# Attention with the two key blocks of a window laid over each other

## The chip, the cores and the metric

The kernel runs on one core of one Trainium2 chip. A core has five engines with queues of their own: TensorE (PE; its weight loads are shown apart as PEld), VectorE (DVE), ScalarE (ACT), GpSimd (POOL) and SyncE (SP, which here issues most DMA transfers). The metric is the device time of one execution in microseconds. Before the change it is 1674.65 us, the median of 3 runs (1673.33 to 1675.32).

## The reference, cut to what matters

One layer of a decoder trunk on 2048 positions of width 1024. A modulated input `u` is multiplied by a wide matrix and split into parts; one of them goes through sliding-window attention with 16 query heads of 64, 2 key/value heads, a bias by distance and one extra "sink" logit per head:

```python
in_window = (dist >= 0) & (dist < WINDOW)          # WINDOW = BLOCK = 128
...
logits = jnp.einsum('bnqhgd,bnkhd->bnhgqk', qb, kb).astype(jnp.float32) * (HEAD_DIM ** -0.5) + bias
logits = jnp.where(mask[None, :, None, None], logits, NEG_INF)
sink = jnp.broadcast_to(sinks.astype(jnp.float32).reshape(N_KV_HEADS, Q_GROUP, 1, 1),
                        logits.shape[:-1] + (1,))
probs = jax.nn.softmax(jnp.concatenate([logits, sink], axis=-1), axis=-1)[..., :-1]
out = jnp.einsum('bnhgqk,bnkhd->bnqhgd', probs.astype(v.dtype), vb)
```

Queries are taken in blocks of 128 and see the block before and their own, 256 keys. With a window of exactly 128, query `q` sees of the block before the keys at places `k > q`, and of its own block those at `k <= q`. So each place `k` from 0 to 127 is used once, either in the one block or in the other. The rest of the layer (gates, a causal pool over 2 to 16 positions, projections, a layer norm) is not touched by the change.

## The kernel before, in words

All large products are made in three passes of a split into a high and a low part (`hi`, `lo`: ACT casts the high part, DVE or POOL subtracts it, line 132 `low`), and by a scheme of sums and differences of matrix quarters, so that each weight tile `W` needs additions on POOL (`sum1` line 266, `mid` lines 270 and 271, `late` line 275) before it is split.

The work is staged: a head, a ring of products for the first 1024 positions (`first_phase`, with the keys and values among them), attention for these (`attention(ph, 0, ...)`, 801), the ring and attention for the second 1024 positions, and a last stage of projections and norms. The instructions of the wrapped engines (`pe`, `act`, `dve`, `pool`, `sp`, class `Ordered`) keep the order in which the program writes them on their engine; those written with `nc.` are placed by the planner.

An attention phase is a loop over `n`, with 64 turns that score and 3 more that finish. A turn stands for two heads and one query block; eight blocks, then the next two heads. Turn `n` writes, in this order:

- PE: the scores of turn `n` (`score_mms`, 992; two heads, high and low keys, 256 keys wide, into one PSUM tile `lg`); the transposes of the probabilities of turn `n - 2` (`turn_mms`, 1006; one per head and key block, into `pt`).
- DVE: the reciprocal of the sums of turn `n - 1`; additions of the output of turn `n - 3` (`o`).
- ACT: the scaling of one head of turn `n - 1`; the high part `pth` of `pt`.
- DVE and ACT: for each head of turn `n`, a reduction that adds the bias `bt` to the scores and finds the extreme (a custom DVE instruction that writes `L`), then the exponential with its sum.
- DVE: the low part `ptl` of `pt`; the scaling of the other head of turn `n - 1`.
- the fill (`filling`, 978): 5 or 6 quarter products, three matmuls of 128x512 each, of the other work that shares the phase. For them `split` (919) writes on ACT a cast, and on POOL or DVE a low part, and on POOL `mid` or `late`; the low part is on DVE for `T1` and for what `on_dve` lists, otherwise on POOL. A split is written three products ahead of its use.
- PE: the value product of turn `n - 2` (`value_mms`, 1013): for both key blocks, `pth` and `ptl` against `vv`, which holds the high and the low part of V side by side.
- what falls due (`run_coming`, 823): among it on POOL the causal pool's sums (`pool_sums`, 830: `nxt`, `fin`), its gate (`take_p`, 858) and the attention gate (`o` by `ag`).

In the first block of the sequence only one key block exists (`k0 = P`), and the turn works on half the columns.

The keys and values of the second kv head are kept in DRAM and loaded over the first at turns 28 to 33. `turn_v` (747) makes `vv` in the ring before: it transposes V, takes the high and low parts, and stores those of the second kv head. `bias_rows` (780) builds on POOL, at the start, one row per head of the bias by distance, filled up with 1e30 outside the window (`ET` = 384 long); `bias_tile` (812) reads it shifted by one per partition.

## Time and profile before

| | |
|---|---|
| median of 3 runs | 1674.65 us |
| the profiled execution's span | 1673.9 us |
| PE busy | 1642.9 us (98%) |
| DVE, ACT, POOL busy | 1205.2, 1024.4, 947.1 us |
| PE on the chain that ended last | 84% of the span |

The span runs from the first to the last instruction of the profiled execution; the median counts what lies around it too and is of other executions. A row of a group gives the engine, the operation, output and input tiles, the shapes, the count, the busy time, the mean time of one in ns, and the idle time ahead with what ended it. Matmuls overlap in the array, so the mean of one is longer than its share of the busy time. A row of a window gives the length and, for each engine, the busy time and the number of instructions, then the granted clock, the share of the DMA engines and GB/s.

### The profile page before, as it was taken

To read this page: it belongs to the slowest core of one execution; us is meant where nothing else is said; L and a number is where in the kernel's file an instruction comes from. 1 tells how busy PE (TensorE), PEld (TensorE's weight loads), DVE (VectorE), ACT (ScalarE), POOL (GpSimd) and SP (SyncE) were. 2 spreads that over 40 slices of the span, in tenths; PEclk is the share of its full clock that TensorE was granted. 3 is DMA by queue.
4 is the path that set the end of the run, shared out by engine and by line. 5 is a ranking of instruction groups with operands and counts; after the bars stand their busy time and mean duration, and the time that the engine had idled before them with its cause. 6 is when DMAs were issued, how large, how long until landed. Compare 5 with 4: busy or idle time off the path is not lost.

```text
span 1673.9 us, 24680 instructions
## 1 busy us (share of the span) xinstructions
PE 1642.9 (98%) x8058; PEld 1383.7 (83%) x8058; DVE 1205.2 (72%) x2156; ACT 1024.4 (61%) x2146; POOL 947.1 (57%) x710
## 2 busy tenths in 40 slices
PE   7999999999999999999999999999999999999997
PEld 6788888888888788888888888888888888888886
DVE  6945646777867767576467677678668897879877
ACT  4754547778777656335477777786656455544552
POOL 3343437585867837873375858588355643433442
PEclk9999999999999999999999999999999999999999
DMA  9588843343543578873432434435869696668443
GB/s 362 209 288 296 209 156 121 100 133 107 164 139 110 177 275 289 326 265 131 143 128 82 145 125 152 145 109 188 301 227 351 241 326 234 225 232 295 152 151 114
DMA packets 185970, 331.56 MB, mean 198 GB/s; under 512 B 18016, under 2 KB 43760, under 8 KB 185840
## 3 DMA queue, kind: packets, MB, share of 16 engines
q1 hardware_dynamic: 182720, 325.72, 56.8%
q10 hardware_dynamic: 3088, 4.23, 1.1%
q8 instruction: 64, 1.05, 0.3%
q14 instruction: 66, 0.54, 0.1%
q0 software_dynamic: 32, 0.02, 0.0%
HBM read 223.77 MB, written 109.28 MB: 199 GB/s over the span
## 4 chain that ended last, share of the span: by engine, by line
PE 84%; DVE 6%; DMA 4%; POOL 2%; issue 2%; ACT 2%; SPq 0%; POOLq 0%; DVEq 0%; ACTq 0%
PE mm L57 53%; PE lg L57 24%; PE pv L57 4%; PE pt L57 4%; DMA head_T<-in_wada_dram 1%; DVE w_set L132 1%; DMA set_T<-ain_T 1%; DVE wide L57 1%; DMA head_B<-in_wada_dram 1%; DVE set_T L57 1%; DVE L L57 1%; DVE w_set L57 0%; ACT L L57 0%; ACT w_set L57 0%; POOL W L270 0%
## 5 line engine op out<-in xcount | busy, mean ns | idle before, releaser
L57 PE MATMUL mm<-set_B,w_set 128*128 128x512 f32 x2664 | 652.1, 392 | 0.1
L57 PEld LDWEIGHTS mm<-set_B,w_set 128*128 128x128 f32 x2664 | 495.9, 188 | 101.9 <-DVE set_B L57 0.7
L57 PE MATMUL mm<-set_T,w_set 128*128 128x512 f32 x1824 | 454.9, 396 | 1.6 <-DVE mm L57 1.2
L57 PE MATMUL lg<-set_T,w_set 128*128 128x512 f32 x1704 | 409.7, 390 | 2.1 <-ACT set_T L57 0.5
L57 PEld LDWEIGHTS mm<-set_T,w_set 128*128 128x128 f32 x1824 | 337.5, 189 | 70.5 <-DVE mm L57 3.3
L57 PEld LDWEIGHTS lg<-set_T,w_set 128*128 128x128 f32 x1704 | 318.4, 188 | 71.9 <-DVE w_set L132 1.6
L132 DVE TENSOR_TENSOR w_set<-W,w_set 128x1024 fp32r<-128x1024 f32 x137 | 194.7, 1423 | 143.9 <-ACT w_set L303 135.3
L303 ACT CAST w_set<-W 128x1024 fp32r<-128x1024 f32 x137 | 144.0, 1051 | 186.2 <-PE mm L57 130.2
L266 POOL TENSOR_TENSOR W<-W,A 128x512 f32<-128x512 f32 x46 | 73.7, 1603 | 260.0 <-DMA A<-in_win_dram 63.6
L57 POOL TENSOR_TENSOR w_set<-W,w_set 128x512 fp32r<-128x512 f32 x120 | 159.0, 1333 | 109.2 <-ACT w_set L57 104.4
L57 DVE TENSOR_TENSOR o<-pv,o 64x128 f32<-64x128 f32 x256 | 72.0, 281 | 96.9 <-ACT o L57 93.6
L57 POOL TENSOR_TENSOR W<-W 128x512 f32<-128x512 f32 x82 | 110.9, 1366 | 52.4 <-DVE sm L57 25.4
L57 ACT ACTIVATE L<-L,nm 128x257 f32<-128x257 f32 (+1 forms) x256 | 127.1, 498 | 18.4 <-DVE nm L57 8.9
L275 POOL TENSOR_TENSOR W<-W 128x512 f32<-128x512 f32 x46 | 70.8, 1540 | 112.3 <-DVE w_set L132 97.6
L270 POOL TENSOR_TENSOR W<-W 128x512 f32<-128x512 f32 x44 | 77.4, 1763 | 83.1 <-DVE w_set L132 70.9
L57 DVE CUSTOM_DVE_ANT_0 L<-lg,bt,nsink 128x256 f32<-128x256 f32 (+1 forms) x256 | 111.6, 473 | 14.4 <-DMA pg<-pg_d 5.1
L57 ACT CAST w_set<-W 128x512 fp32r<-128x512 f32 (+1 forms) x165 | 101.4, 628 | 25.1 <-POOL W L57 14.5
L57 ACT COPY o<-pv 64x256 f32<-64x256 f32 x128 | 47.3, 369 | 71.7 <-PE pv L57 70.5
L57 POOL TENSOR_TENSOR spare<-spare 128x512 f32<-128x512 f32 x48 | 82.8, 1732 | 10.1 <-ACT spare L57 5.8
L57 DVE TENSOR_TENSOR ptl<-pt,pth 128x512 fp32r<-128x512 f32 (+1 forms) x128 | 85.7, 669 | 1.0 <-ACT pth L57 0.9
L57 ACT ACTIVATE L<-L,sm 128x256 f32<-128x256 f32 (+1 forms) x128 | 64.3, 502 | 36.0 <-DVE sm L57 35.6
L271 POOL TENSOR_TENSOR W<-W 128x512 f32<-128x512 f32 x44 | 68.1, 1548 | 29.2 <-DMA W<-in_win_dram 22.0
(234 smaller groups left out, 2408.3 us busy)
## 6 DMA issues: line engine op xcount, KB each, us to landing
W<-in_win_dram SPq DMA_DIRECT2D x42, 512.0 KB, 5.4
W<-in_win_dram SPq DMA_DIRECT2D x42, 256.0 KB, 4.0
A<-in_win_dram SPq DMA_DIRECT2D x42, 256.0 KB, 4.7
ag_d<-sig SPq DMA_DIRECT2D x32, 256.0 KB, 5.9
pg_d<-sig SPq DMA_DIRECT2D x32, 256.0 KB, 4.3
pg<-pg_d SPq DMA_DIRECT2D x32, 256.0 KB, 3.2
pin_B<-fin SPq DMA_DIRECT2D x32, 256.0 KB, 2.0
ag<-ag_d SPq DMA_DIRECT2D x32, 256.0 KB, 3.0
```

Of the source, the lines that this page charges most:

```text
L57: return lambda *args, **kw: self.tc.keep_in_program_order(op(*args, **kw))
L132: engine.tensor_tensor(dst, src, as32(hi), ALU.subtract)
L266: e.tensor_tensor(self.w[:, 1, :], self.w[:, 2, :], self.a22, ALU.add)
L270: e.tensor_tensor(x[:, 1, :], x[:, 1, :], x[:, 0, :], ALU.subtract)
L271: e.tensor_tensor(x[:, 2, :], x[:, 0, :], x[:, 2, :], ALU.subtract)
L275: e.tensor_tensor(x[:, 3, :], x[:, 3, :], x[:, 1, :], ALU.subtract)
L303: a.copy(by_two(hi), raw)
```

## The change

A query block's two score blocks are laid over each other before the softmax. A mask `own` (1 where `k <= q`) is made once; a predicated copy on DVE puts the own block's scores over those of the block before where the mask is 1, in PSUM. Bias rows, bias tiles, reductions, exponentials, scalings, transposes and the splitting into parts then work on 128 columns per head. In the first block (`c0`), the own block's scores are used alone with a bias that a select on POOL fills with 1e30 outside the window.

The value product is `p V_before + p_own (V_own - V_before)`: the probabilities `px` (high and low part) against `vv` of the block before, and `pm`, which is `px` with zeros where the key is not of the own block, against `dv`, the differences of neighbouring V blocks. `pm` is made by a select on POOL (`own_half`). `turn_v` also makes the differences and their parts, stores those of the second kv head, and they are loaded at turns 30 and 33. In the fill, the low parts of `B11` and `T4` are made on DVE for all products.

```diff
-ET = 384
+ET = 256
...
-            turn_v(ph, s, *vts[i])
+            turn_v(ph, s, *sorted(vts, key=lambda v: v[0])[i])
...
     def turn_v(ph, s, t, vt):
+        nonlocal dv
+        if t == 0:
+            dv = kvp.tile([P, 2 * NB, P], F32R, tag="dv", name="dv")
...
+        last = v_last.rearrange("p (a d) -> p a d", a=2)
+        whole, steps = (ph.c(x).rearrange("p (b a d) -> p b a d", b=NB, a=2) for x in ("vw", "vs"))
+        nc.scalar.copy(whole, vtp)
+        nc.gpsimd.tensor_tensor(steps[:, 1:], whole[:, 1:], whole[:, 0 : NB - 1], ALU.subtract)
+        nc.gpsimd.tensor_tensor(steps[:, 0], whole[:, 0], last, ALU.subtract)
+        nc.scalar.copy(last, whole[:, NB - 1])
...
+        for full, src, stored, first in ((vv, vtp, v_d, 1), (dv, steps, dv_d, 0)):
+            blocks = slice(first + NB * t, first + NB * (t + 1))
+            for kv in range(2):
+                dst = ph.c("v1", F32R).rearrange("p (b d) -> p b d", b=NB) if kv else full[:, blocks]
+                parts(dst, src[:, :, kv, :])
+                if kv:
+                    sp.dma_start(stored[s, :, blocks], as32(dst))
...
-            dst = ph.t.tile([P, 2, CH], F32R, tag="k1", bufs=1, name="k1") if kv else kk[:, :, c0 : c0 + CH]
+            dst = kvp.tile([P, 2, CH], F32R, tag="dv", name="k1") if kv else kk[:, :, c0 : c0 + CH]
...
+        def own_half(out, x, fill, blocks, turned):
+            pool.affine_select(
+                out=out,
+                in_=x,
+                compare_op=ALU.is_ge,
+                fill=fill,
+                base=0,
+                pattern=[[0, 2]] * blocks + [[turned, P]],
+                channel_multiplier=-turned,
+            )
...
-        on_dve = set()
+        on_dve = {(x, name) for x in range(K + 2) for name in ("B11", "T4")}
...
-        def turn_mms(L, k0):
-            pt = ps.tile([P, 2, 2, P], F32, tag="pt", bufs=1, name="pt")
-            for hf in range(k0 // P, 2):
-                for h in range(2):
-                    pe.transpose(pt[:, hf, h, :], L[:, h, hf * P : (hf + 1) * P], ident)
+        def turn_mms(L):
+            pt = ps.tile([P, 2, P], F32, tag="pt", bufs=1, name="pt")
+            for h in range(2):
+                pe.transpose(pt[:, h, :], L[:, h, 0:P], ident)
             return pt
 
-        def value_mms(b, k0, pth, ptl):
+        def value_mms(b, px, pm):
             pv = bank("pv")[:, 0 : 2 * P].rearrange("p (h q) -> p h q", h=2)
-            todo = [(hf, x) for x in (pth, ptl) for hf in range(k0 // P, 2)]
-            for n, (hf, x) in enumerate(todo):
-                mm(pv, vv[:, b + hf, :], x[:, hf], start=n == 0, stop=n == len(todo) - 1)
+            todo = [(x[:, u], m[:, b]) for x, m in ((px, dv if pm is None else vv), (pm, dv)) if x is not None for u in range(2)]
+            for n, (x, m) in enumerate(todo):
+                mm(pv, m, x, start=n == 0, stop=n == len(todo) - 1)
             return pv
...
-                pth = tp.tile([P, 2, 2, P], F32R, tag="pth", bufs=1, name="pth")
-                ptl = tp.tile([P, 2, 2, P], F32R, tag="ptl", bufs=1, name="ptl")
-                act.copy(pth[:, h0:], pt[:, h0:])
+                px = tp.tile([P, 2, 2, P], F32R, tag="px", bufs=1, name="px")
+                act.copy(px[:, 0], pt)
...
+                both, bt = lg[:, :, 0:P], bts[j]
+                if c0:
+                    both = lg[:, :, P:]
+                    bt = tp.tile([P, 2, P], F32, tag="pm", bufs=1, name="b0")
+                    own_half(bt, bts[j], BIG, 1, -1)
+                else:
+                    dve.copy_predicated(both, own, lg[:, :, P:])
                 for h in range(2):
                     dve.tensor_tensor_reduce(
-                        L[:, h, c0:256],
-                        lg[:, h, c0:],
-                        bts[j][:, h, c0:],
+                        L[:, h, 0:P],
+                        both[:, h],
+                        bt[:, h],
...
             if pt is not None:
-                low(dve, ptl[:, h0:], pt[:, h0:], pth[:, h0:])
+                low(dve, px[:, 1], pt, px[:, 0])
+                pm = None
+                if not k0:
+                    pm = tp.tile([P, 2, 2, P], F32R, tag="pm", bufs=1, name="pm")
+                    own_half(pm, px, 0.0, 2, 1)
...
             if pt is not None:
-                pvs[n - 2] = value_mms((n - 2) % U, k0, pth, ptl)
+                pvs[n - 2] = value_mms((n - 2) % U, px, pm)
...
+                sp.dma_start(as32(dv[:, 0:NB]), dv_d[s, :, 0:NB])
...
+                sp.dma_start(as32(dv[:, NB:]), dv_d[s, :, NB:])
...
+    nc.gpsimd.memset(own, 1)
+    nc.gpsimd.affine_select(
+        out=own, in_=own, compare_op=ALU.is_ge, fill=0.0, base=0, pattern=[[0, 2], [-1, P]], channel_multiplier=1
+    )
```

## The prediction

> **What bounds the kernel now.** First the page: TensorE (PE) is busy almost throughout, so time comes from PE's own work or from PE being made to wait.

> ```profile
> span 1673.9 us, 24680 instructions
> PE 1642.9 (98%) x8058; PEld 1383.7 (83%) x8058; DVE 1205.2 (72%) x2156; ACT 1024.4 (61%) x2146; POOL 947.1 (57%) x710
> ```

> Then the table by stage, for the two attention phases, from the first score product to the last value product (columns: window; length and PE busy; PEld, DVE, ACT, POOL busy; clock; DMA share; GB/s).

> ```profile
> 256.40:594.80 338.40, 334.75 (x1809) 287.51 (x1808) 244.69 (x668) 256.81 (x715) 247.64 (x200) 0.99 0.41 134
> 828.70:1174.10 345.40, 342.73 (x1870) 295.32 (x1871) 253.13 (x674) 262.11 (x717) 247.87 (x194) 1.00 0.41 135
> ```

> PE idles 3.65 and 2.67 us in 684. The other engines have room on average: POOL 73%, DVE 73%, ACT 76%. Each phase runs 64 score steps (67 turns of the loop); a turn takes 338.4/64.5 = 5.2 us. One turn in PE's timeline, and VectorE (DVE) in it:

> ```profile
> 446.60 0.40 PE L57 MATMUL pv<-pth,vv 128*128 128x256 f32 x2
> ...
> 447.07 0.63 PE L57 MATMUL lg<-kk,qs 128*128 128x256 f32 x4
> 447.54 0.60 PE L57 MATMUL pt<-ident,L 128*128 128x128 f32 x4
> 447.90 1.64 PE L57 MATMUL mm<-set_T,w_set 128*128 128x512 f32 x6
> 449.37 2.20 PE L57 MATMUL mm<-set_B,w_set 128*128 128x512 f32 x9
> 451.41 0.40 PE L57 MATMUL pv<-pth,vv 128*128 128x256 f32 x2
> ```
> ```profile
> 448.05 0.58 DVE L57 TENSOR_TENSOR o<-pv,o 64x128 f32<-64x128 f32 x2 [1.21 <-ACT o L57]
> 448.67 0.48 DVE L57 CUSTOM_DVE_ANT_0 L<-lg,bt,nsink 128x256 f32<-128x256 f32 x1
> ...
> 449.48 0.68 DVE L57 TENSOR_TENSOR ptl<-pt,pth 128x512 fp32r<-128x512 f32 x1
> ```

> Scores, transposes, 15 (or 18) fill products, value products, with no gap. The low half of the turned probabilities (ptl) is there at 450.16, PE wants it at 451.65: what prepares the value product has some 1.5 us to spare, no more.

> **The change part by part.** These are the groups that it touches, forms kept apart (busy us, mean ns), and three rows for its new POOL work.

> ```profile
> L57 PE MATMUL pt<-ident,L 128*128 128x128 f32 x496 | 75.5, 272 | 0.1
> ...
> L57 DVE CUSTOM_DVE_ANT_0 L<-lg,bt,nsink 128x256 f32<-128x256 f32 x240 | 106.7, 482 | 10.0 <-DMA pg<-pg_d 5.1 <-PE lg L57 1.2
> L57 DVE CUSTOM_DVE_ANT_0 L<-lg,bt,nsink 128x128 f32<-128x128 f32 x16 | 5.0, 348 | 4.4 <-DMA bt<-e_rep 4.2
> ...
> L57 DVE TENSOR_TENSOR ptl<-pt,pth 128x512 fp32r<-128x512 f32 x120 | 82.3, 686 | 1.0 <-ACT pth L57 0.9
> L57 DVE TENSOR_TENSOR ptl<-pt,pth 128x256 fp32r<-128x256 f32 x8 | 3.4, 419 | 0.0
> ...
> L57 DVE TENSOR_TENSOR w_set<-W,w_set 128x512 fp32r<-128x512 f32 x40 | 36.5, 914 | 23.6 <-ACT w_set L57 23.3
> ...
> L57 POOL TENSOR_TENSOR w_set<-W,w_set 128x512 fp32r<-128x512 f32 x120 | 159.0, 1333 | 109.2 <-ACT w_set L57 104.4
> ```
> ```profile
> masks.py:199 POOL TENSOR_SCALAR_AFFINE_SELECT ident<-ident x1: 291/291/291, 1.0 to 1.0; 128x128 f32<-128x128 f32 x1
> ```
> ```profile
> L1688 POOL MEMSET const-float32-0.0<- 128x1 f32 x1 | 0.1, 103 | 0.2 <-issue 0.2
> ...
> L57 POOL TENSOR_TENSOR fin<-fin,fix 128x16 f32<-128x16 f32 x8 | 2.1, 263 | 0.6
> ```

> Removed on PE: 120 turns have four transposes and keep two, the 8 turns of a first block have two already. 240 of 496 go, at 75.5/496 = 0.152 us of PE time each: **36.5 us**, all on the bounding engine, 0.30 us a turn. Scores keep their count and width. The value product has four products a turn before (hi, lo by two blocks) and four after (hi, lo by V, hi, lo by the difference): nothing.

> DVE, each turn: the two bias reductions lose 2 x (482 - 348) = 0.27 us, the low half 686 - 419 = 0.27. The predicated copy is not in the trace: between the 0.35 us of a 128x128 reduction and the 0.69 of a 512-wide subtraction from PSUM; I take 0.42, the 256-wide one. The chain to the low half becomes 0.12 us shorter, which by itself is off PE's path. ACT has less of everything (casts, exponentials, scaling of 128 columns for 256); it is not the bound, so nothing.

> New on POOL: one select of 512 elements in each of the 120 turns (`own_half` on px). The one select in the trace takes 0.291 us for 128. By proportion 512 cost 1.16; with the 0.263 that a tiny POOL operation takes as the fixed part, 0.37; with the 0.103 of the one-column memset, 0.103 + 4 x 0.188 = **0.86**, which I take, a select being the single-input kind. [...]

> Moved from POOL to DVE: the low halves of B11 and T4 in the fill, 25 a phase (14 + 13, less two already there). POOL loses 25 x 1.33 = 33 us and gains 60 x 0.86 = 52; it goes from 248 to 267 of some 330 us, 81%. DVE gains 25 x 0.91 = 23 and loses 60 x 0.12 = 7: 253 + 16 of 345, 78%. On average neither is a bound.

> But POOL runs its instructions in the order written, and **the select of turn n stands behind all that POOL got in the turns before it, and the value product of turn n now waits for it**. Before, PE needed POOL's results (fill low halves) only some two turns later, so a backlog cost nothing. From the turn shown: the low half is now there 2.97 us after the turn's start (450.16 - 447.07 = 3.09, less 0.12), the select at 3.9 with 0.05 to hand over. PE comes to the two masked products 0.30 us earlier than it came to the value product and 0.24 after it begins: 4.3 us in a 15-product turn, 5.0 in an 18-product one, 4.6 on average. So 0.7 us to spare, and between two selects POOL has 5.2 - 0.30 - 0.9 = 4.0 us for other work, 4.6-4.7 when the turn before was not held. What it has in one turn is uneven. Here are the stretches of POOL work in the first phase that the code issues in one turn (the second and the fourth: in two turns) and that exceed this; POOL busy is the fifth busy figure:

> ```profile
> 269.33:275.42 6.09, 6.09 (x36) 5.26 (x35) 4.27 (x11) 4.38 (x13) 6.08 (x6) 1.00 0.30 102
> 351.62:364.35 12.73, 12.73 (x74) 11.18 (x73) 7.90 (x23) 10.40 (x29) 12.42 (x12) 1.00 0.38 117
> 373.41:378.90 5.49, 5.49 (x32) 4.76 (x32) 4.37 (x12) 4.11 (x11) 5.49 (x5) 1.00 0.55 185
> 431.06:444.77 13.71, 13.51 (x74) 11.54 (x74) 11.40 (x31) 11.10 (x33) 12.28 (x12) 1.00 0.27 77
> 447.29:456.09 8.80, 8.80 (x50) 7.61 (x49) 7.94 (x19) 6.31 (x20) 8.64 (x9) 1.00 0.52 173
> 459.05:465.47 6.42, 6.42 (x36) 5.51 (x35) 4.69 (x17) 5.89 (x19) 6.34 (x7) 1.00 0.50 169
> 522.92:531.36 8.44, 8.44 (x51) 7.40 (x50) 5.88 (x17) 6.63 (x20) 8.13 (x9) 1.00 0.74 218
> 533.96:540.31 6.35, 6.35 (x40) 5.62 (x39) 5.00 (x11) 4.42 (x14) 6.11 (x7) 1.00 0.01 3
> 540.27:550.03 9.76, 9.50 (x51) 7.88 (x50) 7.99 (x23) 8.12 (x23) 9.37 (x10) 1.00 0.51 162
> 552.50:563.65 11.15, 11.15 (x60) 9.55 (x59) 8.21 (x19) 4.63 (x14) 10.91 (x10) 1.00 0.56 166
> ```

> PE is held by what is over 4.6 (8.6 for two turns; 4.0 for 540.27, right behind a held one), after taking off the moved low halves (two in 447.29 and 552.50, one in 522.92, at 1.33): 1.5 + 3.8 + 0.9 + 3.7 + 1.4 + 1.7 + 2.2 + 1.5 + 5.4 + 3.6 = 25.7 us. The second phase has the same order of work and as much POOL time: **51 us** in both.

> A hold also costs clock. Before, PE waited 2.0 us in all here:

> ```profile
> 567.02 0.50 PE L57 MATMUL pv<-pth,vv 128*128 128x256 f32 x2 [1.39 <-ACT pth L57]
> 568.15 0.51 PE L57 MATMUL pv<-ptl,vv 128*128 128x256 f32 x2 [0.63 <-DVE ptl L57]
> ...
> 569.56 5.27 PE L57 MATMUL mm<-set_T,w_set 128*128 128x512 f32 x15
> ```
> ```profile
> 570.00:572.00 2.00, 2.00 (x6) 1.57 (x5) 1.95 (x7) 1.65 (x4) 2.00 (x2) 0.50 0.70 265
> ```

> The granted clock fell to 0.50, and 15 products took 5.27 us for some 3.7 (1.64 + 2.20 in the turn shown, less overlap): 1.6 us more. Five holds a phase are of 2 us or over; while PE is slow POOL catches up, so half: 10 x 0.8 = 8, less the 3.6 us of this old wait and its clock, which the holds contain: 4.4. [...]

> The rest I cost at nothing. The mask and twice the bias operations at the start stand before POOL's first weight sum at 66 us, whose wait for its DMA covers them; the V differences in the stage before each attention (two PSUM copies, four POOL subtractions, two parts more a turn) lie under PE work that is 45.0 of 45 us busy there, and would cost up to 5 us a phase if the five c buffers ran out. The transfers of dv come at turns 30 and 33, four turns before use.

> **Sum:** 1673.9 - 36.5 + 51.4 + 4.4 = 1693.2 for the profiled execution, whose span lies 0.75 us under the median of 1674.65: **1694 us**.

> **The rivals.** *Holds that mostly vanish* (faster). POOL's operations are of two speeds for one form:

> ```profile
> 442.17 1.04 POOL L57 TENSOR_TENSOR fin<-nxt 128x512 f32<-128x512 f32 x1 [1.04 <-DMA pin_B<-fin]
> ```
> ```profile
> 537.70 1.30 POOL L57 TENSOR_TENSOR fin<-nxt 128x512 f32<-128x512 f32 x1
> ```

> If DVE's halved work lets most of them run at the quicker, the some 70 in the stretches (87 by the rows, less the moved ones and the neighbours cut by a window's edge) give back up to 70 x 0.26 = 18 us a phase, and a select at the lower end 12 x 0.5 = 6; then only the 540 stretch holds, and 1675 - 36.5 + 2 x 3 = 1644. It decides once POOL's work in a turn is below 4.6 us. For it: POOL averages under that. Against: the slow ones coincide also with DVE operations that stay. *DVE late* (slower still). A moved low half waits for ACT's cast, as the 23.3 us of waits in 40 of them show, 0.58 each, and stands ahead of the next turn's reciprocal. DVE's spare time is (338.4 - 244.7)/64.5 = 1.5 us a turn; where two fall into one turn (1.83 + 0.58) the low half comes 0.9 late. With half of the 50 exposed at (0.91 + 0.58): 37 us less the 0.7 spare in each: 1694 + 20 = 1714. *A wash*: holds and gain cancel, 1675; this would take holds of 36 us.

> **How the numbers follow.** Forecast 0.52 (its own range 1680 to 1712), holds vanish 0.27, DVE late 0.13, wash 0.08. 0.2% of 1675 is 3.3 us, about what a measurement can tell. Faster 0.27, same 0.08, slower 0.65. Low end 1646: just above the first rival. High end 1734: select at 1.16 (24 held turns x 0.3 = 7), DVE late, full clock loss (8).

> **What would show it.** Right: in the attention phases PE waits at `pv` for POOL `pm`, some 40 us or more, most at the turns listed; 256 transposes left; clock 0.5 in places. Wrong: PE waits for `pm` under 20 us; a select far from 0.86 us; waits at `pv` or the fill put down to DVE (px, w_set) instead; new waits in the stage of the V transposes.

## The result, and the profile after

The changed kernel takes 1736.3 us (median of 4 runs, 1734.3 to 1739.43) where the kernel before, in 4 runs beside it, takes 1674.28 us (1673.33 to 1675.32): a ratio of 1.037 (95% interval 1.0356 to 1.0385), 62 us slower. The prediction was 1694 us, slower; the direction is right, the size is three times the forecast.

The page of the changed kernel, with the chain that ended last by engine in the third row:

```profile
span 1734.3 us, 24556 instructions
PE 1646.5 (95%) x7818; PEld 1373.9 (79%) x7818; DVE 1216.8 (70%) x2335; ACT 965.0 (56%) x2162; POOL 988.6 (57%) x829
...
PE 31%; DVE 7%; POOL 6%; issue 4%; ACT 2%; DMA 1%; POOLq 0%; SPq 0%; DVEq 0%; ACTq 0%
```

240 matmuls are gone and PE is as long busy as before. The table by stage, the two attention phases (columns as in the prediction):

```profile
259.70:633.90 374.20, 341.18 (x1727) 287.03 (x1726) 253.10 (x755) 229.09 (x718) 259.00 (x241) 0.97 0.38 123
861.70:1234.10 372.40, 343.59 (x1742) 289.92 (x1743) 257.78 (x763) 228.84 (x718) 257.42 (x232) 0.97 0.38 124
```

Before, the phases took 344.0 and 345.5 us, so they are longer by 30.2 and 26.9. (The first window of the prediction's table, 338.4 us, stops 5.6 us short of that phase's last value product; the mean turn before is 5.2 us all the same.) The first score product starts at 259.7 us for 256.4 (+3.3), and the two stages behind the phases are within 0.6 us of what they were. PE idles 33.0 and 28.8 us in the phases, for 3.7 and 2.7. The view of waits says for what (columns: total us, times, longest):

```profile
PE pv L57 <- POOL pm L57: 45.6, 34, 5.3
PE mm L57 <- DVE mm L57: 13.9, 7, 2.5
POOL pm L57 <- DVE px L57: 100.7, 56, 6.6
```

The first is the wait that the prediction named: the value product for the masked probabilities. The third shows that POOL, at the same instruction, waits twice as long for its own input, in 56 turns: it is late in some turns and early in the others. The second wait is one that the forecast left out.

The groups that answer to those shown of before (busy us, mean ns, idle ahead):

```profile
L57 PE MATMUL pt<-ident,L 128*128 128x128 f32 x256 | 50.2, 278 | 0.0
...
L57 DVE COPY_PREDICATED lg<-own,lg 128x256 f32<-128x256 int8 x120 | 49.3, 410 | 3.9 <-PE lg L57 3.9
...
L57 DVE CUSTOM_DVE_ANT_0 L<-lg,bt,nsink 128x128 f32<-128x128 f32 x240 | 74.8, 349 | 4.5 <-DMA bt<-e_rep 0.2
...
L57 DVE TENSOR_TENSOR px<-pt,px 128x256 fp32r<-128x256 f32 x128 | 53.9, 421 | 0.3
...
L57 POOL TENSOR_SCALAR_AFFINE_SELECT pm<-px 128x512 fp32r<-128x512 f32 x120 | 80.8, 674 | 113.6 <-DVE px L57 100.7
```

The copy (0.42 forecast), the reductions and the low part are as costed. The select is 0.67, not 0.86. The transposes went from 75.5 us to 50.2, by 25.3 and not by 36.5.

Where a hold comes from, in the first phase: PE's two masked products of the turn that starts at 463.7 (listed in the prediction as 447.29:456.09), and POOL's order ahead of them:

```profile
470.13 0.50 PE L57 MATMUL pv<-pm,dv 128*128 128x256 f32 x2 [1.86 <-POOL pm L57]
```
```profile
464.60 1.30 POOL L57 TENSOR_TENSOR fin<-fin,pg 128x512 f32<-128x512 f32 x1 [3.26 <-DVE sm L57]
465.86 1.06 POOL L57 TENSOR_TENSOR nxt<-vb 128x518 f32<-128x518 f32 x1
466.99 1.05 POOL L57 TENSOR_TENSOR nxt<-nxt 128x516 f32<-128x516 f32 x1
468.12 1.37 POOL L57 TENSOR_TENSOR fin<-nxt 128x512 f32<-128x512 f32 x1
469.44 0.63 POOL L57 TENSOR_SCALAR_AFFINE_SELECT pm<-px 128x512 fp32r<-128x512 f32 x1
```

Four operations of the causal pool, which nobody needs at once, stand ahead of the select; POOL itself had been idle 3.26 us just before. The hold two turns earlier, and what the clock did behind both (windows; the clock is the third figure from the right):

```profile
456.53 0.50 PE L57 MATMUL pv<-pm,dv 128*128 128x256 f32 x2 [3.95 <-POOL pm L57]
...
457.48 4.58 PE L57 MATMUL mm<-set_B,w_set 128*128 128x512 f32 x12
```
```profile
457.80:461.00 3.20, 3.20 (x9) 2.43 (x9) 2.45 (x9) 1.86 (x7) 2.71 (x3) 0.50 0.49 168
...
471.40:474.40 3.00, 3.00 (x8) 2.32 (x7) 2.88 (x10) 2.34 (x8) 1.80 (x2) 0.50 0.10 39
```

In the two phases the clock falls to 0.50 ten times, eight times for 3.4 us and twice for 6.8 (before: once, for 3.4). PE works in 37.4 of these 40.9 us, so some 18.7 us of work are lost, for 1.7 before.

The second wait: PE wants the sum of a finished quarter (`close`, the row that ends on `mm<-mm,p`) out of the accumulator, and on DVE two moved low parts stand ahead of it, each of which waits for ACT's cast. PE first, then DVE:

```profile
611.07 1.50 PE L57 MATMUL mm<-set_T,w_set 128*128 128x512 f32 x3 [2.53 <-DVE mm L57]
```
```profile
607.70 1.60 DVE L57 TENSOR_TENSOR w_set<-W,w_set 128x512 fp32r<-128x512 f32 x1 [0.72 <-ACT w_set L57]
...
609.71 0.69 DVE L57 TENSOR_TENSOR w_set<-A,w_set 128x512 fp32r<-128x512 f32 x1 [0.41 <-ACT w_set L57]
610.32 0.69 DVE L57 TENSOR_TENSOR mm<-mm,p 128x512 f32<-128x512 f32 x1
```

The head, before and after: POOL builds the bias rows with twice the instructions, and ACT's cast into `set_T` comes 3.6 us later, after a wait that is new.

```profile
9.22 12.82 POOL L57 TENSOR_SCALAR head_T<-head_T 16x1 f32<-16x1 f32 x32 [7.56 <-DMA head_T<-in_relT_dram]
...
38.16 0.62 ACT L57 CAST set_T<-head_qs 128x512 fp32r<-128x512 f32 x1 [1.08 <-issue]
```
```profile
8.52 27.91 POOL L57 TENSOR_SCALAR head_T<-head_T 16x1 f32<-16x1 f32 x64 [6.55 <-DMA head_T<-in_relT_dram]
...
41.74 0.62 ACT L57 CAST set_T<-head_qs 128x512 fp32r<-128x512 f32 x1 [4.74 <-DMA e_d<-head_T]
```

The rows are built in a tile with the tag `set_T2` (`room` in `bias_rows`), so the cast that takes this space next has to wait until their transfer to `e_d` has read it.

### The profile page after: what moved, and what is told of

Same layout as the page of the kernel before. It is cut to its first block, busy times and chain, and to the rows that moved or that the text cites. A ratio compares the mean times of both kernels' runs of the same rounds, so it can differ in the third digit from the quotient of the medians.

```text
span 1734.3 us, 24556 instructions
## 1 busy us (share of the span) xinstructions
PE 1646.5 (95%) x7818; PEld 1373.9 (79%) x7818; DVE 1216.8 (70%) x2335; ACT 965.0 (56%) x2162; POOL 988.6 (57%) x829
## 4 chain that ended last, share of the span: by engine, by line
PE 31%; DVE 7%; POOL 6%; issue 4%; ACT 2%; DMA 1%; POOLq 0%; SPq 0%; DVEq 0%; ACTq 0%
PE mm L57 19%; PE lg L57 11%; POOL nxt L57 1%; POOL fin L57 1%; POOL W L57 1%; DVE w_set L135 1%; PE pv L57 1%; ACT L L57 1%; DVE qs L57 1%; POOL pm L57 1%; DVE wide L57 1%; DVE o L57 1%; DVE w_set L57 1%; ACT w_set L57 1%; POOL o L57 0%
## 5 line engine op out<-in xcount | busy, mean ns | idle before, releaser
L57 PE MATMUL mm<-set_B,w_set 128*128 128x512 f32 x2664 | 661.2, 396 | 0.9 <-DVE w_set L57 0.5
L57 PEld LDWEIGHTS mm<-set_B,w_set 128*128 128x128 f32 x2664 | 502.0, 190 | 106.2 <-DVE set_B L57 1.2
L57 PE MATMUL mm<-set_T,w_set 128*128 128x512 f32 x1824 | 460.3, 399 | 14.4 <-DVE mm L57 13.9
L57 PE MATMUL lg<-set_T,w_set 128*128 128x512 f32 x1704 | 410.6, 391 | 4.1 <-ACT w_set L57 2.2
L57 PEld LDWEIGHTS mm<-set_T,w_set 128*128 128x128 f32 x1824 | 339.9, 191 | 86.0 <-DVE mm L57 15.9
L57 PEld LDWEIGHTS lg<-set_T,w_set 128*128 128x128 f32 x1704 | 319.6, 188 | 73.7 <-ACT w_set L57 2.8
L57 POOL TENSOR_TENSOR w_set<-W,w_set 128x512 fp32r<-128x512 f32 x92 | 121.4, 1325 | 47.6 <-ACT w_set L57 47.4
L57 DVE TENSOR_TENSOR o<-pv,o 64x128 f32<-64x128 f32 x256 | 71.9, 281 | 108.4 <-ACT o L57 105.7
L57 POOL TENSOR_SCALAR_AFFINE_SELECT pm<-px 128x512 fp32r<-128x512 f32 x120 | 80.8, 674 | 113.6 <-DVE px L57 100.7
L57 ACT ACTIVATE L<-L,nm 128x129 f32<-128x129 f32 x256 | 101.4, 398 | 78.2 <-DVE nm L57 75.4
L57 DVE TENSOR_TENSOR w_set<-W,w_set 128x512 fp32r<-128x512 f32 (+1 forms) x73 | 80.0, 1096 | 71.9 <-ACT w_set L57 69.5
L57 POOL TENSOR_TENSOR W<-W 128x512 f32<-128x512 f32 x82 | 109.2, 1345 | 31.9 <-DVE w_set L57 19.7
L57 ACT CAST w_set<-W 128x512 fp32r<-128x512 f32 (+1 forms) x165 | 101.6, 628 | 29.8 <-POOL W L57 12.4
L57 ACT COPY o<-pv 64x256 f32<-64x256 f32 x128 | 47.3, 370 | 116.6 <-PE pv L57 115.1
L57 PE MATMUL pv<-pm,dv 128*128 128x256 f32 x240 | 53.9, 307 | 45.8 <-POOL pm L57 45.6
L57 POOL TENSOR_TENSOR spare<-spare 128x512 f32<-128x512 f32 x48 | 82.6, 1728 | 11.4 <-ACT spare L57 5.7
```

The source lines that it names most:

```text
L57: return lambda *args, **kw: self.tc.keep_in_program_order(op(*args, **kw))
```

## The experiments

All edits are against the changed kernel, and the diffs are shortened. The kernel before took 1674.3 to 1675.5 us beside each of them.

**1. Without the wait.** The masked products take `px` in place of `pm`; the selects still run, but nobody waits for them. The mask of the value product is left out of the computation.

```diff
-                pvs[n - 2] = value_mms((n - 2) % U, px, pm)
+                pvs[n - 2] = value_mms((n - 2) % U, px, pm and px)
```

> Changed kernel; the select still runs in every turn, but the last two value products of a turn take px in place of pm, so PE doesn't wait for POOL (the attention output leaves out the mask of the own block). Theory 'order' (PE is held because the select stands behind POOL's backlog): the 46 us of PE waits for pm go, and with them some 6 of the 10 drops of the clock (1.7 us each): 1736 - 46 - 11 = about 1679, 1670 to 1690. Rival 'load' (POOL has too much work, whoever waits for it): the fill's low halves come late in place of pm, and the time stays above 1715.

Measured: 1693.5 us (ratio 1.0113, 1.0098 to 1.0128), 3.5 us above the range of 'order' and far below the rival's 1715. The wait at `pm` and what hangs on it cost 43 us. PE still idles 18.3 and 15.6 us, now mostly for DVE:

```profile
PE mm L57 <- DVE mm L57: 17.5, 7, 6.9
```

**2. Without the selects too.** `own_half(pm, ...)` goes and `pm = px`; the same part is left out.

> As the run before, and the 120 selects are left out too (the attention output leaves out the mask of the own block). 'Order': within 6 us of the run that has the selects without the wait, 1670 to 1685. 'Load': 20 us or more below it. If DVE's waits (mm<-set_T waiting for a DVE addition, 14 us in the changed kernel) are of DVE's own making, they are still there.

Measured: 1682.2 us (1.004, 1.0025 to 1.0055), 11 us less than with the selects, between the two expectations. So the selects cost PE time beyond the wait for them; the fill's waits for DVE fall to 8.5 and 8.4 us from 12.6 and 10.8. One part of the path is in the two traces: the same DVE operations take 517.8 us in the phases with the selects and 505.9 without (the last section has more on this). How much of the 11 us it makes was not measured.

**3. And the low parts of B11 and T4 back on POOL**, the same part of the mask left out:

```diff
-        on_dve = {(x, name) for x in range(K + 2) for name in ("B11", "T4")}
+        on_dve = set()
```

> No select, and the low halves of B11 and T4 back on POOL (the attention output leaves out the mask of the own block). What is left of the change is fewer transposes and less work of DVE and ACT. If the two low halves in one turn on DVE make PE wait for DVE's additions: 15 to 22 us below the run without select (14 us of waits and some 4 drops of the clock), about 1655. If DVE's lateness came from POOL's selects: within 5 us of it.

Measured: 1660.0 us (0.9908, 0.9891 to 0.9925), 22 us less again, and faster than before. The phases:

```profile
260.20:596.25 336.05, 330.31 (x1727) 280.06 (x1726) 240.57 (x730) 229.28 (x720) 253.20 (x212) 0.99 0.42 137
825.30:1160.35 335.05, 330.23 (x1742) 281.09 (x1743) 243.51 (x738) 228.30 (x718) 248.18 (x194) 1.00 0.42 138
```

This is what laying the blocks over each other is worth if the mask costs nothing: 15 us, with 11 us of idle PE and the head's 3.8 (first score at 260.2 us) still in it.

**4. The low parts back on POOL, with the mask.** The changed kernel with the edit of 3 alone; the whole computation.

> Changed kernel with the low halves of B11 and T4 back on POOL, selects and waits as they are. 'Order': POOL has 50 x 1.33 = 66 us more ahead of its selects, in the turns of most work two operations more, PE waits for DVE 14 us less: 1736 + 40 - 20, 1740 to 1775. Rival 'DVE late' (the move is what costs): 1712 to 1725.

Measured: 1727.7 us (1.0317, 1.0302 to 1.0333), between the two expectations. The two effects of the move are both there and oppose each other: the waits for DVE's `close` nearly vanish, and those for `pm` grow from 45.6 to 54.1 us.

```profile
PE pv L57 <- POOL pm L57: 54.1, 34, 4.9
...
PE mm L57 <- DVE mm L57: 1.7, 2, 0.9
```

So the move to DVE did relieve POOL (by 8.5 us of waits) and cost more than that: 9 us net with the selects, 22 without them.

**5. The mask on DVE.** A multiplication by a tile of ones and zeros in place of the select, with the low parts back on POOL and the bias rows built once (as in 7); the whole computation.

```diff
-                    own_half(pm, px, 0.0, 2, 1)
+                    dve.tensor_tensor(pm, as32(px), keep, ALU.mult)     # keep repeated 4 times
```

> The whole computation. The mask of the own block is a multiplication on DVE (a 128x128 tile of ones and zeros, repeated) right behind the low half, in place of POOL's select; the low halves of B11 and T4 are back on POOL; the bias rows are built once and copied. Theory 'order': no instruction of POOL stands before the value product any more; against the run without select and with the low halves on POOL (1660) it has 120 DVE multiplications of about 0.69 us more, DVE at some 85% in the attention phases, and 3.5 us less in the head: 1656 to 1672, faster than the kernel before. Rival: DVE becomes the bound that POOL was, every turn 0.7 us late: over 1690.

Measured: 1702.1 us (1.0159, 1.0144 to 1.0174), above the rival's 1690. One multiplication takes

```profile
L57 DVE TENSOR_TENSOR pm<-px,keep 128x512 fp32r<-128x512 f32 x120 | 115.4, 962 | 4.1
```

and the waits for `pm` fall to 16.2 us, 28 times. The 42 us above experiment 3 are not all in waits that name the mask: 9.3 us are waits for `close` again, and 6.0 of them come in one turn of the first phase. In the two phases PE idles 35.2 us for 10.6, and its value products take 93.4 us for 83.6, its transposes 54.7 for 49.9. The 46 multiplications beside which POOL ran no two-input operation took the expected 0.69 us; the other 74 took 1.13 on average. So the mask on DVE is not free of POOL either.

**6. The value product later.** The select stays on POOL, and the value product goes behind the scores and transposes of the next turn, to give the select a turn's start more; low parts back, bias rows once; the whole computation.

```diff
-            if pt is not None:
-                pvs[n - 2] = value_mms((n - 2) % U, px, pm)
+            if n - 3 in ready:                     # right behind turn_mms of turn n
+                pvs[n - 3] = value_mms((n - 3) % U, *ready.pop(n - 3))
...
+                ready[n - 2] = px, pm
```

> The whole computation, select on POOL. The value product of a turn stands behind the next turn's scores and transposes (0.63 + 0.25 us of PE work later) in place of the end of its own turn; low halves back on POOL, bias rows built once. 'Order': each of the some 37 waits for pm gets 0.9 us shorter or goes: 54 - 30 = some 25 us of waits are left and half of the clock's drops; from 1727.7: 1727.7 - 30 - 8 - 3.5 = 1686, 1675 to 1698. Rival 'load': as the run with the low halves back, 1720 to 1728.

Measured: 1796.4 us (1.072, 1.0702 to 1.0738), missing both expectations. The edit brought waits of its own:

```profile
PE pv L57 <- DVE o L57: 107.2, 82, 3.2
```

The value product now writes the one `pv` bank just when DVE is about to add the one before to `o`, and ACT's next `px` waits for the product (145.2 us in 115 waits). The wait for POOL's `pm` did fall to 9.2 us, but with PE held elsewhere POOL has more time in any case, so this run does not test the theory. Putting the product a whole turn later would need second buffers of `px` and `pm`; it was not tried.

**7. The bias rows once.** One instruction per bucket, and a copy of the whole row; the whole computation.

```diff
-            for a in range(2):
-                pool.tensor_scalar(et[:, a, t0:t1], ...)
+            pool.tensor_scalar(et[:, 0, t0:t1], ...)
+        pool.tensor_copy(et[:, 1, :], et[:, 0, :])
```

> Changed kernel with the bias rows built once on POOL (32 small operations in place of 64) and copied. If the head's 3.3 us are ACT's wait for the DMA that reads the bias rows out of the space of set_T2: first score product near 256 us again and the whole 3 to 4 us shorter, 1732.5. Rival (the head's start varies with its DMA): no difference.

Measured: 1734.5 us (1.0353, 1.0337 to 1.0368). In the profile the first score is at 256.1 us again, 3.6 earlier, and the phases (373.7 and 372.3) stay. The medians differ by 1.8 us only, and the two ranges overlap, so the gain is shown in the profile and not in the time.

**8. Every transpose twice,** on top of experiment 3 (the mask left out): four transposes in a turn again.

```diff
-            for h in range(2):
+            for h in (0, 1, 0, 1):
                 pe.transpose(pt[:, h, :], L[:, h, 0:P], ident)
```

> The run without select and with the low halves on POOL (it leaves out the mask of the own block), with each transpose made twice into the same place: four per turn as before the change, and nothing else. It measures the disputed term. By the PE timeline (0.36 us from the first of four transposes to the next product, 0.14 of two) 128 turns cost 0.20 to 0.22 us each: 1660 + 26 to 28 = 1687. By the group's busy time over its count (the prediction's 0.152 us each, 256 of them): 1660 + 39 = 1699.

Measured: 1678.7 us (1.0025, 1.0016 to 1.0035): 18.7 us more than experiment 3, under both expectations. Turns in which PE never waits take 4.81 us (15 products) and 5.49 (18), as in the kernel before, for 4.61 and 5.29 with half the transposes: 0.20 us a turn, 25.6 us for 128 turns. Against this, waits go under the added work: PE idles 6.0 us in the phases for 10.6, and the clock no longer falls (once in experiment 3, 1.7 us). It also says what the other parts are worth together: with four transposes, no mask and the low parts where they were, the changed kernel lies 4 us above the kernel before, and 3.8 of these are the head's (first score at 260.2 us); its two phases take 689.6 us, where the kernel before takes 689.5. The halved exponentials, scalings and reductions, the predicated copy and the V differences come to about nothing.

**9. The mask on DVE, one scaling moved to ACT.** Experiment 5 with DVE's scaling of the second head put on ACT; the whole computation.

```diff
-dve.tensor_scalar(E[:, 1, 0:P], E[:, 1, 0:P], sm[:, 1:2], None, ALU.mult)
+act.activation(E[:, 1, 0:P], E[:, 1, 0:P], AF.Copy, scale=sm[:, 1:2])
```

> The whole computation. The run with the mask on DVE, with the second head's scaling of the probabilities (128 operations, 663 ns in that run, 85 us) moved from DVE to ACT (0.40 each). If that run's 42 us over the one without a mask are DVE's lateness (115 us of multiplications on an engine 83% busy in the phases), two thirds to three quarters of them go: 1702 - 30 = 1672, 1664 to 1682. Rival (the mask itself is late for the product, whatever else DVE does): 1695 or more. ACT then stands at some 72% and could be late itself.

Measured: 1694.8 us (1.0124, 1.0111 to 1.0138), 7 us less; the expectation by DVE's load had 1664 to 1682, and the rival 1695 or more. The waits for `pm` stay at 16.0 us in 28 turns, so most of what the mask costs on DVE does not depend on this load.

**10 and 11. Mixed.** DVE makes the mask in the 22 turns of a phase in which POOL has much to do, POOL in the others; 11 with the scaling on DVE, 10 with it on ACT; low parts back, bias rows once; the whole computation.

```diff
-                    own_half(pm, px, 0.0, 2, 1)
+                    if n in FULL:      # 3, 6, 8, 11, 13, 19, 20, 23, 24, 31, 32, 34, 35, ...
+                        dve.tensor_tensor(pm, as32(px), keep, ALU.mult)
+                    else:
+                        own_half(pm, px, 0.0, 2, 1)
```

> The whole computation. The mask is a multiplication on DVE in the 22 turns of each phase in which PE waited for POOL's select or for the turn before such a wait, and POOL's select in the others; low halves back on POOL, bias rows once, second head's scaling on ACT. 'Order': the waits of the select come from POOL's turns of most work alone, so nearly all of them go without DVE's load of 120 multiplications: 1660 - 4 + 5 to 15 = 1661 to 1671, below the kernel before (1674.5). Rival 'load': the selects cost wherever they stand, over 1680.

> As the run before, with the second head's scaling on DVE as it was. It tells the two moves apart: if the choice by turn does the work, within 6 us of it; if ACT's relief of DVE does, 15 us or more above it. 'Order': 1665 to 1678.

Measured: 1712.3 us (1.0225, 1.0211 to 1.0239) and 1705.2 us (1.0185, 1.0171 to 1.0199); both miss the numbers of 'order', 10 lies where its rival 'load' had it (over 1680), and here the scaling on ACT loses 7 us where it gained 7 in experiment 9. In 11 the waits are

```profile
PE pv L58 <- POOL pm L58: 25.4, 15, 2.9
...
PE pv L58 <- DVE pm L58: 5.7, 13, 1.0
```

Of the 15 that name POOL 13 are in turns right behind a listed one (2.6 us in turn 21, 2.3 in turn 38, 2.0 in turn 54 of the first phase), and two in the last turn of a phase. What POOL had in the listed turn is not done when it ends, and the first select after it stands behind the rest.

**12. Mixed, with the turns behind the listed ones on DVE too** (38 of 60 turns a phase).

> The whole computation; as the mixed kernel with the scaling on DVE (1705 us), but the mask is made by DVE also in the turns right behind the listed ones (38 of 60 turns a phase instead of 22), by POOL's select in the other 22. Theory (backlog): in the mixed kernel the 25.4 us in which PE waited for POOL's pm (15 times) are selects that stand behind the remainder of POOL's work of the turn before; with these on DVE the waits for POOL's pm fall below 8 us, and those for DVE's pm rise from 5.7 to some 10 to 13 us (with all masks on DVE they were 16.2). The time is 1705 - 17 x 1.2 (with the clock's part) + 7 = about 1692 us, 1686 to 1698. Rival (load on DVE): what is taken off POOL comes back on DVE in the same turns, since splits, sums and scalings of both engines fall into the same turns; the time is 1700 to 1708, no better than with all masks on DVE (1702), and the waits for DVE's pm rise to some 16 us.

Measured: 1700.4 us (1.0159, 1.0145 to 1.0172).

```profile
PE pv L58 <- DVE pm L58: 12.7, 24, 1.1
PE mm L58 <- DVE mm L58: 9.3, 4, 6.1
...
PE pv L58 <- POOL pm L58: 7.2, 4, 2.2
```

The waits are where the theory put them (7.2 us for under 8, 12.7 for 10 to 13), the four left lying in turn 22, the next turn behind 21, and again in the last turn of each phase. The time is the rival's: 11 us of waits for `pm` less, 4 us more for `close`, and 5 us gained. So the backlog is what places the waits, and moving the mask to DVE gives most of the relief back there.

No kernel with the whole computation beat the kernel before: every place tried for the mask costs some 35 us or more over experiment 3 (POOL 68, mixed 40 to 52, DVE 42, DVE with a scaling moved 35), and the gain to be had was 15. (All of these but the first have the bias rows built once, which experiment 3 has not.) The most direct test of the order was not made: the causal pool's sums written behind the select of their turn, or spread over several turns.

## Why the prediction was right or wrong

The profiled span grew by 60.4 us. PE's time in the two phases by what it works on, out of the two traces, beside the prediction's terms:

| term | forecast | measured |
|---|---|---|
| transposes (`pt`, busy) | -36.5 | -25.3 |
| idle at `pm` | +51.4 | +45.6 |
| idle at `mm` for DVE | 0 | +14.4 |
| other idle time, less the old waits | in the clock's term | -4.5 |
| fill products slower (`mm`, busy) | +4.4 | +13.3 |
| value and score products (`pv`, `lg`, busy) | 0 | +15.1 |
| head, other stages | 0 | +3.4 |
| sum | +19.3 | +62.0 |

(The measured sum is 1.6 over the span's growth, since neighbouring products overlap and are counted in both groups.)

The hold came much as forecast. What failed is the sum around it, in three terms: the transposes' saving (36.5) was 11 us too large, the moved low parts, for which PE waits 14.4 us, stood at nothing, and the 4.4 us for an interrupted PE are 28.4 (the two rows 13.3 and 15.1).

**The hold at `pm`: right in mechanism and mostly in place, near in size.** 45.6 us where 51.4 were forecast, and 20.7 of the first phase's 24.9 in the turns of eight of the ten windows listed (269, 351, 373, 431, 447, 522, 540, 552), with the largest at 540 (forecast 5.4, measured 5.3, and 5.0 in the second phase). The other two listed (459, 533) gave 0.4 and 0.7 us for 1.7 and 1.5, the one at 552 gave 1.5 for 3.6, and 3.1 us came in turns that were not listed, so that the sums lie so close is in part luck. Experiment 1 shows that it is this wait: 43 us go with it. On average POOL was indeed no bound: 69% busy in the phases. The select's price was off (0.67 for 0.86), which by the prediction's own 24 held turns is worth 4.6 us.

**"240 of 496 go, at 75.5/496 = 0.152": the size was wrong.** Busy time over count spreads the time in which a transpose overlaps its neighbours over all of them. The right price is from start to start: before, the first of four transposes, busy for 0.60 us together, and the next fill product are 0.36 us apart (447.54 to 447.90 in the prediction's rows). After:

```profile
291.67 0.64 PE L57 MATMUL lg<-kk,qs 128*128 128x256 f32 x4
292.14 0.38 PE L57 MATMUL pt<-ident,L 128*128 128x128 f32 x2
292.28 1.63 PE L57 MATMUL mm<-set_B,w_set 128*128 128x512 f32 x6
```

0.14 us, so two transposes are worth 0.22 and a turn 0.20, where 0.30 was forecast. The remaining ones look dearer by busy over count (50.2/256 = 0.196), though nothing about them changed. The number was to be had from the trace of before. With it the forecast would have been 10 to 12 us slower.

**The move of the low parts, costed by averages alone, was the second error.** It was added to DVE's load ("78%") and then to nothing in the sum, with its cost left to the rival *DVE late* (chance 0.13). That rival happened together with the forecast, not in place of it: 14.4 us of waits, 22 us of time in experiments 2 and 3. It named the right cause, a low part that waits for ACT's cast, and the wrong one behind it: not the reciprocal, but `close`, which PE waits for directly.

**"A hold also costs clock": too small at 4.4 us.** The clock alone lost 18.7 - 1.7 = 17 us; the half that POOL was to catch up in is not seen. Beside the clock, a hold between the second and the third of four value products parts a stream that overlapped: `pv` is 12.4 us longer. The trace of experiment 3, where the four run on, has 83.6 us of `pv` in the phases, the kernel before 82.5, the changed one 94.9. Only 5.3 us of the 94.9 lie in stretches at half clock, so the clock makes some 2.6 of the 12.4. The parting makes the rest: at full clock the four take 0.64 us where they run on (74 turns) and 0.94 where they are parted (40 turns, before 9). Of `mm`, 27.8 us lie at half clock (before 3.4), which makes 12.2 of its 13.3.

**"The mask and twice the bias operations at the start ... whose wait for its DMA covers them": wrong.** The cover for POOL held, but the space did not: the rows' tile shares its memory with `set_T2`, and ACT waited for that. Experiment 7 takes it back: 3.6 us in the profile.

**Right at nothing:** the V differences in the ring (the two stages behind the phases changed by less than 0.6 us), the transfers of `dv`, the predicated copy and the shorter reductions (experiment 8).

**The other rivals.** *Holds that mostly vanish* needed POOL's work in a turn below 4.6 us; the holds came. *A wash* needed holds of 36 us and no other loss.

## What to carry to other kernels

For a new wait on an engine that works in the order written (as POOL from 464.60 to 469.44 above), count what the program writes ahead of the awaited instruction, turn by turn; the engine's average says nothing (POOL, 69% busy in the phases, held PE 34 times), and relief in one turn only moved the hold to the next while the backlog lasted (13 of the 15 waits for POOL in experiment 11). Price removed matmuls from start to start in the timeline, not by busy time over count (0.20 us a turn here for 0.30), and price an operation moved to another engine by who stands behind it there. Before work on a tile at the start is called covered, look whose memory it is.

## What the runs showed of the hardware

**One form, several prices.** The moved low part took 1.60 us on DVE at 607.70 and 0.69 at 609.71 for the same shape and types. The trace shows what goes with it: of the 140 subtractions of this form in the changed kernel, the 61 beside which POOL ran no two-input operation took 0.70 us on average, the other 79 took 1.28 and up to 1.85. (In the kernel before, 44 took 0.69 and 46 took 1.25; for the mask's multiplication see experiment 5.) Why it is so is not shown. The select of 512 elements took 0.67 us where 128 took 0.29, so by these two rows an estimated 1.0 ns for each further element.
